# Values of two live pairs behind the scores, and a later turn for the first weights, in the sampled attention of a FoX and mLSTM decoder step

## The chip, the cores and the metric

The kernel runs on one core of one Trainium2 chip. The time is that of one execution on the device, in microseconds (us). The median of three runs is quoted, and one further execution was taken with the hardware profiler. TensorE (PE) does the matrix products, PEld is its loading of weights, VectorE (DVE) and ScalarE (ACT) work on vectors, GpSimd (POOL) does small vector work and issues the indirect transfers, and SyncE (SP) issues the plain ones.

## The reference: what is computed

One step of a decoder layer runs for 2048 prompt tokens and for eight sampled sequences of eight new tokens each. Both go through one input projection, forgetting attention (FoX, 8 heads of 64) beside an mLSTM matrix memory, one output projection, a norm, a squared-ReLU MLP (1024 to 4096 to 1024) and a second norm. All values are float32. The part that the change touches is the attention of the sampled tokens over 8192 cached positions, which lie in pages that a table names:

```python
def _fox_sample(q, k_new, v_new, logf_new, k_past, v_past, logf_past):
    ...
    s_past = jnp.einsum('bqhd,bkhd->bhqk', q, k_past).astype(jnp.float32) * scale
    s_past = s_past + Ln[..., :, None] + R[:, :, None, :]
    s_new = jnp.einsum('bqhd,bkhd->bhqk', q, k_new).astype(jnp.float32) * scale
    ...
    p = jax.nn.softmax(jnp.concatenate([s_past, s_new], axis=-1), axis=-1).astype(v_new.dtype)
    o = jnp.einsum('bhqk,bkhd->bqhd', p[..., :P], v_past) + jnp.einsum('bhqk,bkhd->bqhd', p[..., P:], v_new)
```

## The kernel before

The program is a main stream with a second one woven into it. The main stream has four parts in order: the input projection with the gates (to about 911 us of the profiled span), the prompt's attention (to about 1340), the output projection (to about 1600) and the MLP (to the end). Every main product is written as two or three matrix products of split operands (`mm3`, L156 to L159; the splitting is done by `split_hi` on ACT at L149 and `split_lo` on DVE at L152). In the MLP the products are named `ph` (hidden layer, evicted by ACT) and `py` (output, added by DVE at L1489).

The second stream is the attention of the eight sampled sequences. It is a Python generator, `sample_attention` (L1531), whose 294 steps (`step`, L1841) are emitted one at a time by `tick` (L129) when the main stream has issued a certain estimated time of matrix work, 5 us for a step in the last two parts. `beside` (L114) places what a step emits on PE, ACT and DVE behind the last main instruction of that engine. Within these bounds a scheduler, which reckons with its own model of the times, puts the instructions of each engine in their final order; instructions on POOL and SP are bound by their data and buffers alone. The stream stands still during the prompt's attention.

For each of the eight sequences (a batch `b` in the code, 32 steps long) the stream does the following.

- **Keys.** `k_gather` (L1666) issues one indirect gather of 512 KB of cached keys on POOL, `k_turn` (L1670) transposes it in place on DVE (L1674). In the later parts of the kernel six such pieces fit into a ring, so that a gather waits until the scores have read the piece whose place it takes.
- **Scores.** Every fourth step `qk_step` (L1683) multiplies the queries with four pieces (L1697, 16 products in 32 instructions of 32 columns, four of them side by side on the array), and DVE adds the forget terms and keeps maxima (L1704). This result is `sQ`.
- **Softmax.** At step 35 of the batch `softmax` (L1709) takes the scores of the new keys (L1716), the maximum, and eight exponentials on ACT (L1734), in four tiles `S` by two head groups, and two small ones of the new keys `Sn` (L1736).
- **Weights.** `weights(b, u, hg)` (L1758) turns a quarter `u` of one head group by four transposes on PE (L1766) into `sT`, and DVE and ACT copy them into `PTs` (L1768). There is one tile `PTs`, which serves four pairs of values.
- **New keys.** `softmax_new` (L1738) sums the exponentials on DVE and transposes those of the new keys (L1746, L1748), `v_new` (L1771) loads the new values (SP, 16 KB), `softmax_sum` (L1750) makes the sums of all pages by a product (L1754) and the reciprocal (L1756). All of it is used at the batch's last pair.
- **Values.** `v_gather` (L1775) issues two gathers of 512 KB, which the code calls a pair. There are two places for pairs: `vt`, and a second one (`vx` or `xr`) that exists only in the output projection and in the MLP, and is withdrawn at the ends of their blocks, where the same buffers take other data. `vx["live"]` lists the places in use, `vx["of"]` the pairs gathered. `pv_step` (L1792) multiplies one pair with the weights (L1809, eight products in 16 instructions) into the accumulator `sO`; the 16th pair of a batch (`kt` 15) adds the new values (L1815) and evicts. `pv_end` (L1820) transposes the result (L1824).

`sQ` and `sT` share a single PSUM buffer (tag `sX`): scores, transposes, new keys and sums take turns on it, each waiting until the one before was read. `at(n, first, of)` (L1833) gives `i` at step `first + i * of`, and nothing at the others. Before, the pair `p` is multiplied at step 38 + 2p: pairs with an even number meet a scores' step, those with an odd number stand two steps later. The first weights (`u` = 0) of a batch stand at its steps 36 and 37, the first in one step with the last pair of the batch before, the new keys at 37 and the sums at 40.

Of the kernel before, what the change touches and what calls it, by code (L numbers as in the profile page):

```python
# [1530 lines left out]
def sample_attention(tc, I, O, ps_, pps, cst, ident, sqk, dnl, dR, dmix, dqb, vx, kx, pe, ring_a):  # L1531
# [84 lines left out]
    for g in range(2):  # L1616
        p = pps.tile([32, 8, 64], F32, name="sT", tag="sX", bufs=1)
# [26 lines left out]
    def q_load(b):  # L1644
        qt = ps_.tile([128, 2, 16, 8], F32, name="qt", bufs=2)
        for n in range(2):
            SY.dma_start(qt[:, n].rearrange("p d t -> p (d t)"), dap(dqb, (n * NB + b) * 4096, [[0, 4], [128, 32], [1, 128]]))
        bn = ps_.tile([128, 2, 8], F32, name="bn", bufs=2)
        for hg in range(2):
            SY.dma_start(bn[:, hg], dap(dnl, hg * 4 * TOT + S + b * 8, [[TOT, 4], [0, 32], [1, 8]]))  # L1650
        state[b] = dict(qt=qt, bn=bn, U=[])
# [18 lines left out]
    def k_turn(n):  # L1670

        for i in range(2):
            x = piece(n)[:, i * 512:(i + 1) * 512]
            V.transpose(x, x)  # L1674
# [8 lines left out]
    def qk_step(g):  # L1683

        b, kt = divmod(g * 2, 16)
        z = state[b]
        rb = z["rb"]
        a0 = piece(4 * g)
        d = 1 if g < GA else (2 * (g - GA) + 1) % 3 - 2 * (g - GA) % 3
        pq = pps.tile([128, 2, 256], F32, name="sQ", tag="sX", bufs=1)  # L1690
        for hg in range(2):
            for db in range(2):
                for h4 in range(4):
                    hd = (hg * 4 + h4) * 2 + db
                    kv = bass.AP(tensor=a0.tensor, offset=a0.offset + hd * 32,
                                 ap=[list(a0.ap[0]), [d * 2048, 2], [512, 4], [1, 32]])
                    r = T.matmul(pq[h4 * 32:h4 * 32 + 32, hg].rearrange("p (k f c) -> p k f c", k=2, f=4), z["qb"][:, hd], kv,  # L1697
                                 start=(db == 0), stop=(db == 1), skip_group_check=True)
        if kt % 4 == 0:
            z["U"].append(ps_.tile([128, 2, 4, 4, 32], F32, name="S", tag="S", bufs=4))  # L1700
        for k in range(2):
            c = slice(k * 128, k * 128 + 128)
            for hg in range(2):
                V.tensor_tensor_reduce(out=z["U"][kt // 4][:, hg, :, kt % 4 + k], in0=pq[:, hg, c].rearrange("p (b t) -> p b t", t=32),  # L1704
                                       in1=rb[:, hg, c].rearrange("p (b t) -> p b t", t=32), scale=1.0, scalar=NEG,
                                       op0=OP.add, op1=OP.max, accum_out=z["mx"][:, hg, kt + k:kt + k + 1])
        return r
# [30 lines left out]
    def softmax_new(b):  # L1738

        z = state[b]  # L1740
        rs = z["rs"] = ps_.tile([128, 2], F32, name="rs", bufs=2)
        V.tensor_reduce(rs, z["rp"], axis=AX.X, op=OP.add)
        pn = z["pn"] = ps_.tile([8, 2, 32], F32, name="PTn", bufs=2)
        p = pps.tile([8, 2, 128], F32, name="sT", tag="sX", bufs=1)
        for hg in range(2):
            T.transpose(p[:, hg], z["Sn"][:, hg], ident)  # L1746
        for hg in range(2):
            A.copy(pn[:, hg].rearrange("p (h q) -> p h q", q=8), p[:, hg].rearrange("p (h g q) -> p g h q", g=4, q=8)[:, 0])  # L1748
# [9 lines left out]
    def weights(b, u, hg):  # L1758

        z = state[b]  # L1760
        if hg == 0:
            z["PT"] = ps_.tile([128, 2, 4, 4, 4, 8], F32, name="PTs", tag="PTs", bufs=1)
        PT = z["PT"]
        p = pps.tile([128, 4, 128], F32, name="sT", tag="sX", bufs=1)
        for f in range(4):
            T.transpose(p[:, f], z["U"][u][:, hg, f].rearrange("p k t -> p (k t)"), ident)  # L1766
        for f in range(4):
            (A.copy if f % 2 else V.tensor_copy)(PT[:, hg, f].rearrange("p g h q -> p h g q"),  # L1768
                                                 p[:, f].rearrange("p (h g q) -> p h g q", g=4, q=8))
# [22 lines left out]
    def pv_step(b, kt, after):  # L1792


        z = state[b]
        if kt == 0:
            z["po"] = pps.tile([128, 256], F32, name="sO", bufs=1)
        po = z["po"]
        pg = kt % 4
        vts = vx["of"].pop(b * 16 + kt)  # L1800
        vx["live"].pop(0)
        for n, f in enumerate((1, 0)):
            with ExitStack() as es:
                if after is not None:
                    es.enter_context(tc.issue_after(after.ins))
                for g in range(2):
                    for hg in range(2):
                        r = (g * 2 + hg) * 32
                        after_ = T.matmul(po[r:r + 32], z["PT"][:, hg, 2 * f + g, pg].rearrange("p h q -> p (h q)"),  # L1809
                                          vts[f][:, g, hg * 256:(hg + 1) * 256], start=(kt == 0 and n == 0),  # L1810
                                          stop=(g == 1 and kt == 15 and n == 1), skip_group_check=True)
            after = after_
        if kt == 15:
            for hg in range(2):
                T.matmul(po[hg * 32:hg * 32 + 32], z["pn"][:, hg], z["vn"][:, hg * 256:(hg + 1) * 256],  # L1815
                         start=False, stop=True, skip_group_check=True)
            z["os"] = ps_.tile([128, 256], F32, name="os", bufs=1)
            V.tensor_scalar(z["os"], po, z["rl"], None, op0=OP.mult)

    def pv_end(b):  # L1820
        z = state.pop(b)
        p = pps.tile([128, 2, 128], F32, name="sT", tag="sX", bufs=1)
        for c in range(2):
            T.transpose(p[:, c], z["os"][:, c * 128:(c + 1) * 128], ident)  # L1824
        for hh in range(2):
            s = slice(hh * 64, hh * 64 + 64)
            for c in range(2):
                for hg in range(2):
                    V.tensor_reduce(mixs[s, hg * 2 + c, b * 8:b * 8 + 8],
                                    p[s, c].rearrange("p (e g h q) -> p g h q e", e=2, g=2, q=8)[:, hg, 2 * c + hh],  # L1830
                                    axis=AX.X, op=OP.add)

    def at(n, first, of):  # L1833

        i, r = divmod(n - first, of)
        return i if r == 0 and i >= 0 else None
# [4 lines left out]
    def step(n):  # L1841
        after = None
        if n == 0:
            q_load(0)
        g, r = divmod(n - 2, 4)
        if 0 <= g < GA and r >= 2:
            k_turn(4 * g + 2 * r - 4)
            k_turn(4 * g + 2 * r - 3)
        if NA + 2 < n < 258:
            if n == NA + 3:  # L1850
                k_turn(NA)
            k_turn(n - 2)
        g = at(n, 6, 4)
        if g is not None and g < 64:
            after = qk_step(g)
        b = at(n, 35, 32)
        if b is not None and b < 8:
            softmax(b)
        p = at(n, 38, 2)
        if p is not None and p < 128:  # L1860
            pv_step(p // 16, p % 16, after)
        b = at(n, 69, 32)
        if b is not None:
            pv_end(b)
        b = at(n, 37, 32)
        if b is not None and b < 8:
            softmax_new(b)
            v_new(b)
        b = at(n, 40, 32)
        if b is not None and b < 8:  # L1870
            softmax_sum(b)
        for hg in range(2):
            u = at(n, 36 + hg, 8)
            if u is not None and u < 32:
                weights(u // 4, u % 4, hg)
        b = at(n, 30, 32)
        if b is not None and b < 7:
            q_load(b + 1)
        b = at(n, 3, 32)
        if b is not None and b < 8:  # L1880
            q_begin(b)
        g = at(n, 4, 4)
        if g is not None and g < 64:
            r_load(g)
        if n >= 35 and (n % 2 == 1 or not vx["live"]):
            while v_room():
                v_gather()
        g, r = divmod(n - 2, 4)
        if 0 <= g < GA and r < 2:
            k_gather(4 * g + 2 * r)  # L1890
            k_gather(4 * g + 2 * r + 1)
        if NA + 6 <= n < 256:
            k_gather(n)

    for n in range(294):
        yield 1
        step(n)
        if n == NA + 2:

            yield 3  # L1900
            for i in range(6):
                k_gather(NA + i)
                if i < 5:
                    yield 1
# [23 lines left out]
```

## Time and profile before

| what | value |
|---|---|
| median of three runs (lowest to highest) | 3322.77 us (3321.24 to 3331.57) |
| the profiled execution | 3348.73 us |
| its span, first to last instruction | 3347.0 us |
| mean granted clock of TensorE | 0.989 |
| DMA | 646.22 MB, 193 GB/s on average |
| gathers issued on POOL for keys and values | 256 and 256 |

The profile gives for each engine its busy time, for each wait the instruction that ended it, and the instructions in order of time. Instructions are named by line, engine, operation and tiles (`sO<-vt,PTs`: the accumulator from a gathered pair and the weights). The recorded ends of matrix products overlap their successors, so that their starts are the better measure. Every float32 product of the sampled stream shows as two instructions: 32 of them for a scores' step, 16 for a pair of values.

### The profile page before, as it was taken

How to read it: one execution, taken by the hardware profiler on the slowest of the kernel's cores; microseconds unless marked ns; L12 is line 12 of the kernel's file. 1: busy time of each engine (PE TensorE's matmuls, PEld its weight loads, DVE VectorE, ACT ScalarE, POOL GpSimd, SP SyncE). 2: the span in 40 equal slices, each digit the busy share in tenths (PEclk: the TensorE clock that was granted, in tenths of full speed). 3: DMA queues.
4: the chain of work that ended last, by engine and by line, in shares of the span. 5: the costliest groups of instructions: out<-in, count | busy, mean ns of one | idle time of the engine just before them, and what ended most of it. 6: DMA issues, size and time to landing. Idle time of an engine off the chain costs nothing. (4 is left out here: it accounts for less than half of the span.)

```text
span 3347.0 us, 57284 instructions
## 1 busy us (share of the span) xinstructions
PE 3224.8 (96%) x21420; PEld 2634.7 (79%) x21420; DVE 2130.2 (64%) x5161; ACT 1355.5 (40%) x2670; POOL 929.7 (28%) x1060
## 2 busy tenths in 40 slices
PE   9999999999999999999999999999999999999998
PEld 8998897787877777676777777777776777889997
DVE  6857567556478777656666667666676545755555
ACT  4443344334367777312332333232332333433332
POOL 0112122322344444465323324323243210100001
PEclk9999999999999999999999999999999999999999
DMA  5666765867642223787877768767668654542221
GB/s 174 167 190 190 220 205 189 288 215 226 220 122 84 77 82 114 246 274 242 296 241 250 247 232 298 253 224 270 211 238 304 198 172 142 160 138 79 89 85 66
DMA packets 427294, 646.22 MB, mean 193 GB/s; under 512 B 83149, under 2 KB 320017, under 8 KB 426121
## 3 DMA queue, kind: packets, MB, share of 16 engines
q1 hardware_dynamic: 350184, 363.09, 35.9%
q0 software_dynamic: 74304, 270.57, 22.0%
q10 hardware_dynamic: 2528, 8.91, 0.7%
q8 instruction: 169, 2.77, 0.3%
q14 instruction: 109, 0.89, 0.1%
HBM read 589.63 MB, written 52.83 MB: 192 GB/s over the span
## 5 line engine op out<-in xcount | busy, mean ns | idle before, releaser
L1489 DVE TENSOR_TENSOR y<-y,py 128x512 f32<-128x512 f32 x475 | 320.6, 682 | 313.5 <-PE py L159 276.9
L149 ACT ACTIVATE wh<-wr 128x1024 fp32r<-128x1024 f32 x268 | 279.4, 1056 | 523.7 <-PE py L159 207.1
L1668 POOL DMA_INDIRECT kT<-cache_k,idxK x256 | 269.1, 1051 | 725.5 <-PE sQ L1697 657.7
L159 PE MATMUL ph<-x1h,wl 128*128 128x512 f32 (+1 forms) x1280 | 452.6, 355 | 9.5 <-DVE wl L152 8.3
L157 PE MATMUL ph<-x1h,wh 128*128 128x512 f32 (+1 forms) x1280 | 454.7, 355 | 4.0 <-ACT wh L149 2.2
L158 PE MATMUL ph<-x1l,wh 128*128 128x512 f32 (+1 forms) x1280 | 454.5, 355 | 1.6 <-issue 1.6
L1674 DVE STREAM_TRANSPOSE kT<-kT 128x512 f32<-128x512 f32 x512 | 330.3, 685 | 182.2 <-DMA kT<-cache_k,idxK 171.6
L157 PE MATMUL py<-wh,h 128*128 128x512 f32 x1024 | 407.0, 400 | 4.4 <-DVE y L1487 2.3
L159 PE MATMUL py<-wh,h 128*128 128x512 f32 x1024 | 401.6, 393 | 1.0 <-issue 1.0
L158 PE MATMUL py<-wl,h 128*128 128x512 f32 x1024 | 401.5, 393 | 1.1 <-issue 1.0
L152 DVE TENSOR_TENSOR wl<-wr,wh 128x1024 fp32r<-128x1024 f32 x268 | 336.8, 1263 | 89.2 <-PE ph L159 35.2
L157 PE MATMUL pm<-whi,xhT 128*128 128x256 f32 (+2 forms) x1040 | 303.4, 292 | 3.2 <-issue 2.0
L158 PE MATMUL pm<-wlo,xhT 128*128 128x256 f32 (+2 forms) x1040 | 298.1, 287 | 0.0
L159 PE MATMUL pm<-whi,xlT 128*128 128x256 f32 (+2 forms) x1040 | 297.9, 286 | 0.0
L159 PEld LDWEIGHTS ph<-x1h,wl 128*128 128x128 f32 x1280 | 241.7, 189 | 45.6 <-DVE wl L152 10.5
L157 PEld LDWEIGHTS ph<-x1h,wh 128*128 128x128 f32 x1280 | 241.5, 189 | 42.0 <-issue 4.7
L158 PEld LDWEIGHTS ph<-x1l,wh 128*128 128x128 f32 x1280 | 241.8, 189 | 37.8 <-issue 6.4
L157 PEld LDWEIGHTS py<-wh,h 128*128 128x128 f32 x1024 | 192.5, 188 | 59.4 <-issue 11.9
L159 PEld LDWEIGHTS py<-wh,h 128*128 128x128 f32 x1024 | 192.5, 188 | 46.9 <-issue 5.8
L158 PEld LDWEIGHTS py<-wl,h 128*128 128x128 f32 x1024 | 192.7, 188 | 37.4 <-issue 2.3
L1785 POOL DMA_INDIRECT vt<-cache_v,idxV x158 | 161.5, 1022 | 201.0 <-PE sO L1809 140.2
L157 PEld LDWEIGHTS pm<-whi,xhT 128*128 128x128 f32 (+1 forms) x1040 | 199.1, 191 | 11.5 <-issue 8.8
(420 smaller groups left out, 6627.5 us busy)
## 6 DMA issues: line engine op xcount, KB each, us to landing
wr<-w SPq DMA_DIRECT2D x256, 512.0 KB
wra<-w_in SPq DMA_DIRECT2D x112, 512.0 KB
Rb<-dR SPq DMA_DIRECT2D x128, 128.0 KB
wr<-w_o SPq DMA_DIRECT2D x16, 512.0 KB
xr<-dmix SPq DMA_DIRECT2D x16, 512.0 KB
y<-x_prompt SPq DMA_DIRECT2D x16, 512.0 KB
dx<-y SPq DMA_DIRECT2D x16, 512.0 KB
xr<-dx SPq DMA_DIRECT2D x16, 512.0 KB
```

Of the source, the lines that this page charges most:

```text
L149: last["ACT"] = A.activation(dst, src, AF.Copy, scale=scale)
L152: r = (eng or V).tensor_tensor(dst, src, hi.bitcast(F32), op=OP.subtract)
L157: T.matmul(ps, wh, xh, start=first, stop=False)
L158: T.matmul(ps, wh, xl, start=False, stop=False)
L159: last["PE"] = T.matmul(ps, wl, xh, start=False, stop=stop)
L1489: V.tensor_tensor(y, y, ps, op=OP.add)
L1668: G.indirect_dma_start(out=piece(n), out_offset=None, in_=ck, in_offset=IO(ap=idxK[:, b, j // 2, j % 2:j % 2 + 1], axis=0))
L1674: V.transpose(x, x)
L1785: G.indirect_dma_start(out=vt.rearrange("p f c -> p (f c)"), out_offset=None, in_=cv, in_offset=IO(ap=idxV[:, b, (kt % 4) * 4 + kt // 4, f ...
```

## The change

`pv_step` returns its last instruction. At a step that is due for pair `p`, the pair is multiplied if that was not done before, and where `p` is even and pair `p` + 1 has been gathered already, that one is multiplied directly behind it, in the same step; a counter `done` keeps the odd step from doing it again. Where only one pair is live, everything stays at its step. Within a batch the first weights of both head groups stand at step 37 (before: 36 and 37); the later weights stay at their steps. The new keys and the new values' load go from step 37 to 39, the sums from 40 to 41. Within a step the order of the calls is as before: scores, softmax, values, `pv_end`, new keys, sums, weights, loads, gathers of values, gathers of keys.

```diff
@@ -1816,6 +1816,7 @@
             V.tensor_scalar(z["os"], po, z["rl"], None, op0=OP.mult)
+        return after
 
     def pv_end(b):
@@ -1857,22 +1858,29 @@
         p = at(n, 38, 2)
-        if p is not None and p < 128:
-            pv_step(p // 16, p % 16, after)
+        if p is not None and p < 128 and p >= done[0]:
+            after = pv_step(p // 16, p % 16, after)
+            done[0] = p + 1
+            if p % 2 == 0 and p + 1 in vx["of"]:
+                pv_step(p // 16, p % 16 + 1, after)
+                done[0] = p + 2
         b = at(n, 69, 32)
         if b is not None:
             pv_end(b)
-        b = at(n, 37, 32)
+        b = at(n, 39, 32)
         if b is not None and b < 8:
             softmax_new(b)
             v_new(b)
-        b = at(n, 40, 32)
+        b = at(n, 41, 32)
         if b is not None and b < 8:
             softmax_sum(b)
         for hg in range(2):
             u = at(n, 36 + hg, 8)
-            if u is not None and u < 32:
+            if u is not None and u < 32 and u % 4:
                 weights(u // 4, u % 4, hg)
+            u = at(n, 37, 32)
+            if u is not None and u < 8:
+                weights(u, 0, hg)
@@ -1892,6 +1900,7 @@
+    done = [0]
     for n in range(294):
         yield 1
         step(n)
```

## The prediction

> **What bounds the kernel now.** I read the page first, then the stretches in which the sampled stream runs, then the waits of TensorE and of its weight loads, and last the timeline of TensorE around single visits of the stream.
>
> ```profile
> PE 3224.8 (96%) x21420; PEld 2634.7 (79%) x21420; DVE 2130.2 (64%) x5161; ACT 1355.5 (40%) x2670; POOL 929.7 (28%) x1060
> ```
>
> TensorE is busy for 96% of the span and no other engine for more than 64%. The profiled execution took 3348.73 us, 1.7 more than its span and 26 (0.8%) more than the median of the three runs, 3322.77. The sum below is made in microseconds of the profiled execution; scaled by 0.992 it changes by 0.1, so I take it off the median as it is.
>
> ```profile
> 1340.00:2830.00 1490.00, 1443.37 (x8898) 1091.11 (x8899) 923.48 (x1794) 485.77 (x781) 514.11 (x478) 0.99 0.70 243
> ```
>
> The columns are the stretch, its length, the busy time (instructions) of PE, PEld, DVE, ACT and POOL, the granted clock, the DMA share and GB/s. From 1340 to 2830 the stream runs beside the output projection and the MLP, which is the only time in which two pairs can be live (before 911 there is one place, so no pair is joined there). There PE is busy for 97% of the time. So time is won here only by giving PE less to do, or less to wait for. The waits are small:
>
> ```profile
> PEld sO L1809 <- issue: 19.6, 58, 0.4
> PEld sT L1766 <- PE sO L1809: 5.0, 12, 0.5
> PE sT L1766 <- ACT PTs L1768: 2.9, 1, 2.9
> PE sT L1766 <- ACT S L1734: 2.2, 1, 2.2
> PE sO L1809 <- DMA vt<-cache_v,idxV: 1.5, 2, 0.8
> ```
>
> Each row is who waited, for whom, microseconds in all, times, the longest. PE waits 1.5 us for values that have not landed and 5.1 for the weights' softmax and copies. The first row says that values are entered 58 times with a short gap (0.34 us each) that nothing but the sequence explains: PE comes from other work, not from the scores. The second has 12 visits in which the next weights' transposes follow values directly.
>
> **What a visit costs.** The main matmuls start 0.227 us apart (13 steps in 2.95 us, first two rows below). Rows of the PE timeline are start, length, line, operation, count.
>
> ```profile
> 1907.72 0.39 PE L159 MATMUL ph<-x1h,wl 128*128 128x512 f32 x1
> ...
> 1910.67 0.39 PE L157 MATMUL ph<-x1h,wh 128*128 128x512 f32 x1
> 1910.98 1.93 PE L1697 MATMUL sQ<-kT,qb 128*32 128x256 f32 x32
> 1912.74 1.05 PE L1809 MATMUL sO<-xr,PTs 128*32 128x256 f32 x16
> 1913.71 0.50 PE L158 MATMUL ph<-x1l,wh 128*128 128x512 f32 x1
> ...
> 1915.69 0.39 PE L157 MATMUL ph<-x1h,wh 128*128 128x512 f32 x1
> ...
> 1920.23 0.39 PE L159 MATMUL py<-wh,h 128*128 128x512 f32 x1
> 1920.55 1.07 PE L1809 MATMUL sO<-vt,PTs 128*32 128x256 f32 x16
> 1921.55 0.50 PE L157 MATMUL py<-wh,h 128*128 128x512 f32 x1
> ...
> 1924.45 0.39 PE L157 MATMUL ph<-x1h,wh 128*128 128x512 f32 x1
> ```
>
> The even pair of this group stands behind the scores, the odd pair alone 10 us later. The lone visit, from 1920.23 to 1924.45, holds 13 main matmuls: 4.22 - 13 x 0.227 = **1.27 us**. The part beyond its 1.00 us of matmuls is a later entry (0.32 for 0.227), a later exit and a dozen main matmuls at 0.23 to 0.24. At nine places the schedule already puts both pairs behind the scores:
>
> ```profile
> 1983.40 0.39 PE L157 MATMUL ph<-x1h,wh 128*128 128x512 f32 x1
> 1983.72 1.93 PE L1697 MATMUL sQ<-kT,qb 128*32 128x256 f32 x32
> 1985.47 1.05 PE L1809 MATMUL sO<-xr,PTs 128*32 128x256 f32 x16
> 1986.33 1.05 PE L1809 MATMUL sO<-vt,PTs 128*32 128x256 f32 x16
> 1987.31 0.50 PE L157 MATMUL py<-wh,h 128*128 128x512 f32 x1
> ...
> 1989.25 0.40 PE L159 MATMUL py<-wh,h 128*128 128x512 f32 x1
> ```
>
> From main matmul to main matmul this visit is 3.91 us (1983.40 to 1987.31), the one with one pair 3.04 (1910.67 to 1913.71); the eight steps after take 1.94 and 1.98. The second pair thus costs 3.91 - 3.04 - 0.04 = **0.83 us**, and joining saves 1.27 - 0.83 = **0.44**.
>
> Three times in a batch the odd pair stands together with the transposes of the next weights, which the change leaves where they are:
>
> ```profile
> 1894.73 0.39 PE L159 MATMUL py<-wh,h 128*128 128x512 f32 x1
> 1895.05 1.07 PE L1809 MATMUL sO<-vt,PTs 128*32 128x256 f32 x16
> 1896.05 0.66 PE L1766 MATMUL sT<-ident,S 128*128 128x128 f32 x4
> ...
> 1898.84 0.39 PE L158 MATMUL py<-wl,h 128*128 128x512 f32 x1
> ...
> 1904.28 0.39 PE L159 MATMUL py<-wh,h 128*128 128x512 f32 x1
> 1904.51 0.60 PE L1766 MATMUL sT<-ident,S 128*128 128x128 f32 x4
> ...
> 1907.27 0.39 PE L158 MATMUL py<-wl,h 128*128 128x512 f32 x1
> ```
>
> With 11 main matmuls between its first and last row, the first visit is 4.11 - 11 x 0.227 = 1.61; the transposes alone, with as many, are 2.99 - 2.50 = 0.49. Afterwards there are 0.83 + 0.49 = 1.32, a saving of **0.29**.
>
> **The count.** I followed the PE timeline from 1380 to 2830, where odd pairs 23 to 127 run. Left out are nine that are joined already and those at the ends of blocks, where the second place is withdrawn (pairs 35, 37, 67, 99, 101). 21 of the rest stand alone and 14 with transposes (12 of these have the gap of the row above). The other entries among the 58 are even pairs, of the last batch above all, and visits cut in two.
>
> 21 x 0.44 = 9.2 and 14 x 0.29 = 4.1. Three irregular places (near 2080, 2120 and 2540, where the scores or both pairs stand apart) give 0.6 each, 1.8. Together 15.1 us.
>
> **Gathers.** Both pairs now free their places in one step, so POOL issues all four gathers of values behind one another, after the key gathers, and they must land before the next scores' step. The beginning of a batch shows that already, since there both pairs are joined today:
>
> ```profile
> 1767.76 1.93 PE L1697 MATMUL sQ<-kT,qb 128*32 128x256 f32 x32
> 1778.71 0.94 POOL L1785 DMA_INDIRECT vt<-cache_v,idxV  x1 [0.30 <-issue]
> 1783.35 1.93 PE L1697 MATMUL sQ<-kT,qb 128*32 128x256 f32 x32
> 2602.41 0.95 POOL L1785 DMA_INDIRECT xr<-cache_v,idxV  x1 [0.30 <-issue]
> 2612.19 1.07 PE L1809 MATMUL sO<-xr,PTs 128*32 128x256 f32 x16 [0.55 <-DMA xr<-cache_v,idxV]
> ```
>
> The last gather goes out 10.9 us after its visit's start (1767.76 to 1778.71). The last two rows are the slowest landing after which PE waited here: 9.8 us. So the second pair is there 21 us after the visit, and a scores' step comes every 27 us (two batches' first steps, 1767.76 and 1983.72, are eight steps apart). Only behind a batch's first visit is the next one early (1783.35, 15.6 us later). For five such pairs, which stand with transposes, I count no saving: 5 x 0.29 = 1.5. Worst, PE waits 3 us at each and the gain shrinks by 15. The key gathers keep their place ahead on POOL, since scores end before values; if the values went first, three more issues of 1.25 us each would delay the keys by some 4 us, for which DVE's transposes wait, and main additions behind them on DVE: bounded by a wait of PE of that length, which no row of a paired visit shows, so nothing is taken.
>
> **The moved steps.** The first weights' eight transposes, eight copies (ACT and DVE) stay the same in number; the first half moves by one step, so both halves stand in one step with the transposes of the old batch's output. The new-key sums (a DVE reduction, two transposes, two ACT copies, and SP's load of 16 KB of new values) move by two steps, the sum's matmuls and its reciprocal by one. All of these results are needed at the batch's last pair, 30 steps later, so they hide behind main matmuls: nothing, as a value. SP's load leaves the step in which it waited for the last pair's matmuls and passes no other load of the stream; loads of main weights stood behind it. All these users share one PSUM buffer:
>
> ```profile
> 1750.31 0.38 PE L1824 MATMUL sT<-ident,os 128*128 128x128 f32 x2
> 1755.80 0.38 PE L1746 MATMUL sT<-ident,Sn 128*8 128x128 f32 x2
> 1761.28 0.60 PE L1766 MATMUL sT<-ident,S 128*128 128x128 f32 x4
> ```
>
> These are the old batch's output, the new keys and the second half of the first weights; the first half stands before them. With the new keys' turn (1755.80) taken out, the scores' step at 1767.76 has one user fewer ahead, up to 6 us earlier. That helps gathers, not PE. Bounds: the waits of 5.1 us go (-5), or both halves, now in neighbouring turns, make PE wait as once today:
>
> ```profile
> 1461.21 1.11 PE L1766 MATMUL sT<-ident,S 128*128 128x128 f32 x4 [2.93 <-ACT PTs L1768]
> ```
>
> ```profile
> 1461.00:1464.40 3.40, 3.19 (x10) 2.71 (x11) 1.93 (x4) 1.40 (x2) 0.56 (x1) 0.50 0.60 171
> ```
>
> The stretch behind the wait has a granted clock (third figure from the end) of 0.50 for 3.4 us, which loses 1.7 more, 4.6 in all. The Trainium skill (TensorE: Matmul & The Clock Gate, "What's actually happening") has the clock fall after an idle window of about 3.4 us; by that alone a wait of 2.9 would cost 2.9. The trace shows the clock fallen after 2.93, and the measurement decides.
>
> **Sum.** -15.1 + 1.5 + 0 = -13.6 us: 3322.8 - 13.6 = **3309**, 0.41% faster. A difference under 0.3% (10 us) cannot be told from none here.
>
> **Rivals.** *Only the switches go* (or half of the pairs stay apart). Without the slow dozen, a lone visit costs 1.09 (1920.23 to 1921.55, less 0.227), a joined pair 0.87; 35 x 0.22 = 7.7, if the dozen stays as slow: 3315. The same follows if the schedule keeps every second odd pair alone because it reckons its gather late, and 3323 if it keeps all: then the change doesn't do what it says. For it: the schedule has joined only nine pairs so far. Against: those are emitted two steps apart today, and the slow dozen after the joined visit is no longer than after the single one. By the Trainium skill (TensorEngine Tiling (Array Packing), "Key Properties") a change of tiling mode drains the engine, and a saving of the drain alone would be this rival; the joined rows show more than that. Chance 0.26, 3313 to 3332.
>
> *The first weights stall.* Both halves share one buffer within a step, and ACT is on its eight exponentials just then. If PE waits as at 1461.21 in all eight batches, that is 8 x 4.6 = 37: 3346. From three batches on the gain is gone; from six on the kernel is slower by over 0.3%. For it: the first weights had a wait for the exponentials of 2.2 us in this stretch. Against: the rows above leave 5.5 to 6.5 us between users, and the wait for the new keys' exponentials leaves the chain. Chance 0.14, 3333 and above.
>
> *More than the sum*: waits of 5 to 10 us at the batches' beginnings go too, half clock included. 3297 to 3303, chance 0.08.
>
> **How the numbers follow.** The forecast has 0.52, from 3303 to 3312. Faster by over 0.3%: 0.52 + 0.08 = 0.60; within: 0.26; slower: 0.14. The range from 3298 to 3336 leaves out about 0.03 below and 0.12 above, the greater part of the slow rival.
>
> **What would show it.** Entries of values from other work fall from 58 to about 25; visits with 32 values' matmuls behind the scores rise from nine to over 35, at 3.9 us; waits for values' gathers stay under 5 us in all; PE's busy time in these stretches falls by some 13. A wait at L1766 or L1809 in most batches would prove me wrong, as would an odd pair still standing alone.

## The result and the profile after

| kernel | median of its runs (lowest to highest) | ratio to the kernel before, 95% interval |
|---|---|---|
| before | 3328.2 us (3321.24 to 3332.96, six runs) | |
| after | 3349.11 us (3335.46 to 3357.44, six runs) | 1.0055 [1.0039, 1.007] |

The change made the kernel slower by 0.55%, some 18 us; the forecast was a gain of 14 us. The profiled execution of after took 3335.46 us (span 3333.8), the shortest of its runs, while that of before had been longer than all of its timed runs. Read side by side they have the sign wrong. So a second profiled execution of the unchanged kernel (`e4`, span 3323.5 us, the same order of instructions on every engine) stands for before from here on, and one of the changed kernel (`e3`, span 3342.4 us) beside the first.

The page of after, and the stretch in which two pairs can be live (columns as in the prediction):

```profile
PE 3212.7 (96%) x21420; PEld 2641.3 (79%) x21420; DVE 2121.0 (64%) x5161; ACT 1358.7 (41%) x2670; POOL 931.0 (28%) x1060
```

```profile
1340.00:2830.00 1490.00, 1445.85 (x8932) 1108.88 (x8929) 922.52 (x1796) 487.47 (x780) 516.99 (x478) 0.99 0.70 244
```

The same stretch of the unchanged kernel's second profile:

```profile
1340.00:2830.00 1490.00, 1457.38 (x9005) 1106.24 (x9001) 941.44 (x1810) 493.31 (x787) 515.43 (x478) 0.99 0.70 245
```

PE is busy for 11.5 us less of these 1490 us, but it also gets through 73 matmuls less (8932 for 9005): part of the fall is not less work but more waiting. The waits of after show that both things happened:

```profile
PEld sO L1809 <- issue: 8.7, 25, 0.4
```

```profile
PE py L157 <- ACT h L149: 6.4, 1, 6.4
PE sT L1766 <- ACT PTs L1768: 6.1, 2, 4.0
PE sT L1766 <- DVE mixs L1830: 5.7, 1, 5.7
PE px L1284 <- DVE x1l L152: 5.0, 2, 3.8
PE sO L1809 <- DMA vt<-cache_v,idxV: 3.9, 5, 1.4
PE px L1284 <- DMA xr<-dx: 3.4, 2, 3.0
...
PE sO L1809 <- DMA xr<-cache_v,idxV: 1.7, 3, 1.1
```

The reader is to see two things. Entries of values from other work fell from 58 to 25 (56 in `e4`), just as forecast, and waits for gathered values are 5.6 us in eight places. But there are new or longer waits, the longest of 4.0 to 6.4 us, at one or two places each, and they are of different kinds: a main operand that ACT has split late (`h`, L149), a buffer that ACT has not yet copied (L1768), the output of the sequence before, which DVE has not yet reduced (L1830). None of them repeats from batch to batch.

Where a joined visit stands, it costs what was forecast (timeline of PE in after, start and length in front):

```profile
1813.06 0.39 PE L159 MATMUL ph<-x1h,wl 128*128 128x512 f32 x1
1813.38 1.93 PE L1697 MATMUL sQ<-kT,qb 128*32 128x256 f32 x32
1815.13 1.05 PE L1809 MATMUL sO<-vt,PTs 128*32 128x256 f32 x16
1815.99 1.05 PE L1809 MATMUL sO<-xr,PTs 128*32 128x256 f32 x16
1816.97 0.50 PE L157 MATMUL py<-wh,h 128*128 128x512 f32 x1
```

3.91 us from main matmul to main matmul. There are 33 such visits (nine before), and not all that were joined in the code stay joined. Here the schedule has put main work between the two pairs, and the first pair's values come late besides:

```profile
1827.62 1.93 PE L1697 MATMUL sQ<-kT,qb 128*32 128x256 f32 x32
1830.19 1.07 PE L1809 MATMUL sO<-vt,PTs 128*32 128x256 f32 x16 [0.64 <-DMA vt<-cache_v,idxV]
1833.68 1.07 PE L1809 MATMUL sO<-xr,PTs 128*32 128x256 f32 x16
```

The span can be split into three: the gaps of PE of over 0.15 us, half of the time in which its clock is granted at 0.50, and the rest, which is nearly all work at full pace. They are added up over all of PE's rows and all of the clock's records within the span.

| kernel, its profile | span | gaps | lost to half clock | rest |
|---|---|---|---|---|
| before, second profile (e4) | 3323.5 | 90.3 | 37.8 | 3195.3 |
| after | 3333.8 | 103.5 | 43.2 | 3187.1 |
| after, second profile (e3) | 3342.4 | 111.5 | 48.2 | 3182.7 |
| joined pairs alone (e1) | 3335.5 | 108.7 | 39.1 | 3187.6 |
| moved steps alone (e2) | 3348.8 | 108.0 | 44.7 | 3196.1 |

The joining took 8 to 13 us of work away (rest: 3195.3 to 3187.1, 3182.7 and 3187.6), and the gaps grew by 13 to 21 us. The moved steps alone change no work (3196.1), and add the gaps all the same. Part of the time at half clock falls into gaps and into the span's end, where PE has nothing to do; counted only while PE is busy, it costs 24.7 us in `e4`, 33.0 in after, 36.8 in `e3`, 28.0 in `e1` and 36.7 in `e2`. One profile is one execution: the rest of the first profile of before was 3205.5, 10 us more than that of the second with the same instructions in the same order, and the profiled execution of after lay 14 us below the median of its runs, that of `e1` 9 us above. So the sizes are good to some microseconds, not better, and the verdicts below go by the ratios.

### The profile page after: what moved, and what is told of

Read it like the earlier page. It is cut to its first block, busy times and chain, and to the rows that moved or that the text cites. A ratio compares the mean times of both kernels' runs of the same rounds, so it can differ in the third digit from the quotient of the medians.

```text
span 3333.8 us, 57289 instructions
## 1 busy us (share of the span) xinstructions
PE 3212.7 (96%) x21420; PEld 2641.3 (79%) x21420; DVE 2121.0 (64%) x5161; ACT 1358.7 (41%) x2670; POOL 931.0 (28%) x1060
## 5 line engine op out<-in xcount | busy, mean ns | idle before, releaser
L149 ACT ACTIVATE wh<-wr 128x1024 fp32r<-128x1024 f32 x268 | 278.3, 1056 | 449.7 <-PE py L159 213.6
L1451 ACT ACTIVATE hq<-ph 128x512 f32<-128x512 f32 (+1 forms) x160 | 82.5, 516 | 313.6 <-PE ph L159 242.6
```

Of the source, the lines that this page charges most:

```text
L149: last["ACT"] = A.activation(dst, src, AF.Copy, scale=scale)
L1451: A.activation(hq, ps, AF.Relu)
```

## The experiments

All kernels compute the whole result. The median and the ratio are those of five rounds against the kernel before.

| run | what differs from the kernel before | median, us | ratio, 95% interval |
|---|---|---|---|
| e3 | the whole change, again | 3353.36 | 1.0081 [1.0063, 1.0099] |
| e4 | nothing | 3328.65 | 0.9998 [0.9984, 1.0012] |
| e1 | pairs joined, no step moved | 3327.96 | 1.0003 [0.9991, 1.0015] |
| e2 | steps moved, no pair joined | 3349.41 | 1.005 [1.003, 1.0069] |
| e5 | of the moved steps, the first weights | 3340.32 | 1.0029 [1.0013, 1.0046] |
| e6 | of the moved steps, new keys and sums | 3342.16 | 1.0036 [1.0022, 1.0049] |
| e7 | moved steps in batches 0 and 1 | 3336.58 | 1.0012 [0.9996, 1.0028] |
| e8 | moved steps in batches 2 to 7 | 3338.43 | 1.003 [1.0016, 1.0045] |
| e17 | moved steps in batches 0, 1, 3, 5, 7 | 3346.09 | 1.0047 [1.0031, 1.0062] |
| e18 | moved steps in batches 2, 4, 6 | 3345.05 | 1.0045 [1.0029, 1.0061] |
| e9 | whole change, norm vectors held back | 3346.3 | 1.0042 [1.003, 1.0054] |
| e10 | moved steps, norm vectors held back | 3344.0 | 1.0039 [1.0026, 1.0052] |
| e11 | joined pairs, norm vectors held back | 3328.93 | 0.999 [0.9981, 0.9999] |
| e12 | norm vectors put first, nothing else | 3340.15 | 1.003 [1.0018, 1.0042] |
| e13 | norms' stores issued by POOL, nothing else | 3331.01 | 1.0006 [0.9993, 1.0019] |
| e14 | e10 with those stores | 3342.19 | 1.0038 [1.0024, 1.0051] |
| e15 | e9 with those stores | 3337.68 | 1.0033 [1.0017, 1.0049] |
| e16 | e11 with those stores | 3330.76 | 1.0004 [0.9991, 1.0016] |

**The change taken apart.** Theory M: the moved steps cost. Theory G: the gathers of joined pairs come late. In e1 the three moved steps stand where they stood before; e2 leaves the joining out of the change, these lines above all:

```diff
-            if p % 2 == 0 and p + 1 in vx["of"]:
-                pv_step(p // 16, p % 16 + 1, after)
-                done[0] = p + 2
```

> Only the joining of two pairs, with the first weights, the new keys and the sums at their old steps. If the moved steps are what costs time (theory M), this is the sum of the prediction without them: 10 to 15 us faster than before, ratio 0.996. If the joined pairs cost it, because four gathers of values in a row land late and TensorE waits for them at half a clock afterwards (theory G), this is as slow as the whole change, ratio 1.004 to 1.007, and its waits for gathered values in the output projection and the MLP are over 5 us in its profile.

> Only the moved steps, pairs as before. Theory M: 0.5 to 1% slower than before, with waits of TensorE at the transposes of first weights of 4 us or more, each with 3.4 us of half clock behind it. Theory G: within 0.2% of before.

> The changed kernel once more, unchanged, on the same chip as the others. Both theories: ratio 1.004 to 1.007. Its profile, a second one, should show where a usual execution differs from the profiled one of the result, which was shorter than all of its timed runs: theory G expects more waits for gathered values, theory M more at the transposes; TensorE's busy time about 3212 us in both.

> The kernel before once more, unchanged. Ratio 1.000 within 0.2%. A second profile of it, since the one that the prediction read was 0.8% longer than the median of the runs: if that excess was in TensorE's waits, this span is near 3325 with TensorE idle for about 100 us instead of 122.

The whole loss is there without any joining (1.005), and none without moved steps (1.0003). So M holds as to which part of the change loses. The waits that M expected are not there: PE waits at first weights in two batches of e2's profile, 3.8 us in batch 0 and 2.2 us in batch 2, each in pieces of 2.3 us or less, and not 4 or more. And the joining does not win what it was to win either, though it takes 7.7 us of work off PE: the gaps of e1 are 18 us longer than those of e4.

For this lost gain the profiles speak for G. From the output projection to the end of the stream, PE waits for gathered values 12.2, 13.8 and 13.7 us in the three kernels with joined pairs and no moved steps (e1, e11, e16), and 2.1 to 6.0 us in those with neither (before, e4, e12, e13). That is some 7 us more, of the 8 to 10 us of work that these three save there.

**Which of the moved steps?** F: the first weights, whose halves now meet in one step. K: new keys and sums. D: neither; each new order of the steps re-times all queues, and the parts don't add up.

```diff
-        b = at(n, 37, 32)
+        b = at(n, 39, 32)
...
-        b = at(n, 40, 32)
+        b = at(n, 41, 32)
```

These lines are e6; e5 has the lines on `weights` of the change instead. In e7 and e8 the whole set of moved steps applies to n under 98 (batches 0 and 1) or from 98 on.

> Only the first weights of both head groups at step 37, new keys and sums at their old steps. Theory F (the first weights' place itself makes TensorE wait): about 20 us slower than before, ratio 1.005 to 1.007. Theory K (the later new keys and sums do, because their vector work then stands in front of the main stream's on VectorE): within 0.2% of before. Theory D (no one place: each new order re-times all queues, and its waits with the half clock behind them are spread): between the two, and the parts do not add up.

> Only the new keys and the load of new values two steps later and the sums one step later; first weights at 36 and 37. Theory F: within 0.2% of before. Theory K: ratio 1.005 to 1.007, with the wait of 2.8 us of the mLSTM's product behind the sums near 850 us that all three profiles with the moved steps have. Theory D: between the two.

> All moved steps, but for the first two batches alone, which begin beside the input projection (before 911 us). If the loss of the moved steps is made there (the 2.8 us wait near 850, a wait of the scores for their transposed keys near 580, one half-clock period more in each profile), ratio 1.003 to 1.006; otherwise within 0.2% of before.

> All moved steps, but for the six later batches alone, which begin beside the output projection and the MLP. If the loss is made there, ratio 1.003 to 1.006; otherwise within 0.2% of before. With theory D both halves lose some, and the two losses need not add up to the 0.5% of the moved steps together.

Each half loses (0.29% and 0.36%), together 0.50%; neither F nor K holds by itself. Early and late batches, 0.12% and 0.30%, do add up within their intervals; the 0.12% alone is not clear of nothing.

**Does SP's queue carry it?** Between the same two main matmuls (the 12376th and the 13200th, the beginning of the MLP's third block) e4 takes 231 us and e7 231, but e8, e2 and e6 take 245 to 248. (The first profile of before takes 236 here, and e1, which loses nothing, 242: a long stretch is not yet a loss.) There, in after, ACT stands still for weights that land late. Timeline of ACT in after:

```profile
2431.11 2.99 ACT L149 ACTIVATE wh<-wr 128x1024 fp32r<-128x1024 f32 x3
2450.05 1.06 ACT L149 ACTIVATE wh<-wr 128x1024 fp32r<-128x1024 f32 x1 [15.95 <-DMA wr<-w]
...
2452.29 0.63 ACT L149 ACTIVATE h<-hq 128x512 fp32r<-128x512 f32 x1
```

and the timeline of PE, which waits for that last row:

```profile
2452.97 0.79 PE L157 MATMUL py<-wh,h 128*128 128x512 f32 x1 [6.39 <-ACT h L149]
```

The last split, `h`, stands behind the split of weights (2450.05) in ACT's order, and with it waits for a load that it doesn't need. In e4 ACT waits for the same load too, 7.51 us, but there the split of `h` stands ahead of it:

```profile
2434.85 0.64 ACT L149 ACTIVATE h<-hq 128x512 fp32r<-128x512 f32 x1
...
2447.15 1.06 ACT L149 ACTIVATE wh<-wr 128x1024 fp32r<-128x1024 f32 x1 [7.51 <-DMA wr<-w]
```

So what differs most is ACT's order. The load itself goes out at 2435.46 in e4 and at 2439.15 in after, 3.7 us later, and lands 11.7 us and 10.8 us after that. SP's timeline just ahead of it, in after:

```profile
2435.72 0.33 SPq L145 DMA_DIRECT2D g<-ln_g  x1
2438.02 0.33 SPq L145 DMA_DIRECT2D b<-ln_b  x1
2439.15 0.38 SPq L1255 DMA_DIRECT2D wr<-w  x1
...
2441.39 1.19 SPq L1272 DMA_DIRECT2D xr<-dx  x2
2442.64 0.56 SPq L1255 DMA_DIRECT2D wr<-w  x1
```

and in e4:

```profile
2418.28 0.94 SPq L1272 DMA_DIRECT2D xr<-dx  x2
2428.61 0.34 SPq L145 DMA_DIRECT2D g<-ln_g  x1
2430.31 0.33 SPq L145 DMA_DIRECT2D b<-ln_b  x1
```

The reader is to see that the same loads have changed places: the next block's rows (`xr<-dx`, L1272) stand ahead of the norm's vectors (L145) in e4 and behind them in after, though the change touches neither. Theory Q: this order is the loss. The lines below are the hold of e9 to e11; e12 does the reverse to the kernel before (the row loads follow the vectors):

```diff
-                    gb = vecs(2)
+                    with ExitStack() as es_l:
+                        if ci < 3:
+                            es_l.enter_context(tc.issue_after(last_x[1 - len(CB[ci + 1])].ins))
+                        gb = vecs(2)
```

> The changed kernel, complete, with the norm vectors' loads (L145) held behind the second load of the next block's rows (L1272) on SP's queue at each block's start, which is where the kernel before has them; the changed kernel has them ahead of all four row loads at the third block. Theory Q (the loss comes from SP's order of loads at the blocks' starts, which the moved steps shift): ratio falls from 1.0055-1.0081 to 1.001-1.003, and the stretch of main matmuls 12376-13200 from 243-251 us to 232-238 us. Theory D (any new order re-times all queues; no one place): 1.0045-1.008 as before, the stretch above 240 us.

> The moved steps alone, with the same hold of the norm vectors' loads behind the second row load (moves alone had them ahead of all four at the second and the third block). Q: ratio 1.001-1.003 (from 1.005), stretch 12376-13200 232-238 us (from 245). D: 1.004-1.006, the stretch above 240 us.

> The joined pairs alone, with the same hold (pairs alone had the vectors ahead of all four row loads at the second and the third block). Q: the joining's 9-10 us of TensorE, which waits ate, come out: ratio 0.997-0.999 (pairs alone: 1.0003), faster than both kernels. D: 0.999-1.0015.

> The kernel before, complete, with nothing of the change: only the norm vectors' loads are put ahead of the four row loads on SP's queue at the starts of blocks two to four. Q: ratio 1.002-1.004, the stretch 12376-13200 above 238 us (from 231-236). D: 0.9985-1.0015.

e12, which has nothing of the change, loses 0.30%. That this is the order of the loads alone is not shown: e12 executes PE's instructions in another order than before at over 100 places, and its third block's stretch takes 234 us, where Q had over 238. The hold may give something back to the joined pairs: e11 is at 0.999 where e1 was at 1.0003, with intervals that overlap. But Q doesn't explain the loss. e1 has the vectors ahead of the rows as after has, and loses nothing. The expectation for e10 was wrong in its premise: moved steps alone had the row loads in front already, and the executed order of e10 is that of e2 on every engine. Its 1.0039 is a second measurement of the same program (1.005 the first time). And e9, where the order was mended, still takes 241 us in the third block's stretch and stays at 1.0042.

**Stores that wait for POOL.** Theory S: SP's store of `y_prompt` waits for POOL's add (L177) ahead of weight loads. The stores of the two norms go out from POOL instead, directly behind the add:

```diff
-            SY.dma_start(dx1[t * 128:(t + 1) * 128], xs[t])
+            G.dma_start(dx1[t * 128:(t + 1) * 128], xs[t])
...
```

> The kernel before, complete, with the norms' stores (L1340, L1497) issued by POOL, right behind the add that they wait for (L177), instead of by SP. Theory S (in the changed kernels SP's store of y_prompt waits up to 19 us for POOL's add, and weight loads queued behind it reach ACT's split up to 10 us late): the kernel before has such waits too, of up to 14-18 us, but other loads behind them: 0.998-1.001. Theory D: 0.998-1.003, any order re-times everything.

> The moved steps alone, norm vectors' loads behind the second row load, and the norms' stores issued by POOL. Theory S together with Q: the rest of the loss (1.0039) goes: 0.999-1.0015 against before, the stretch of main matmuls 12376-13200 230-236 us (from 245.6), ACT's waits for weights there (L150 for wr) under 12 us (from 30). Theory D: 1.003-1.005.

> The changed kernel, complete, with the norm vectors' loads behind the second row load and the norms' stores issued by POOL. S with Q: 0.997-1.001 against before (from 1.0042), the joining's 10 us of TensorE come out. D: 1.003-1.006.

> The joined pairs alone with both edits of SP's queue. S with Q: 0.996-0.999 against before, the fastest of all. D: 0.998-1.002.

S falls. With these waits gone, the moved steps are still at 1.0038, and the stretch takes 249 us; ACT still waits 21 us for weights in it, where S had under 12. e13 adds something else: it executes PE's instructions in another order than the kernel before at over 80 places, and loses nothing that can be measured (1.0006).

**Which batches?** Theory P: the softmax of batches 2, 4 and 6 comes 9 to 11 steps ahead of a block's start, and moved steps cost there alone. In e17 and e18 the moved steps apply to the other batches or to these:

```diff
-        b = at(n, 37, 32)
+        b = at(n, 39 if ((n - 35) // 32 not in (2, 4, 6)) else 37, 32)
...
```

> The moved steps alone, and only in batches 0, 1, 3, 5 and 7, whose softmax does not fall just ahead of a block's start; batches 2, 4 and 6 as before. Theory P (the place: the softmax of batches 2, 4 and 6 comes 9 to 11 steps ahead of the first block's, the third's and the rest of the blocks' loads, where ACT has no time to spare; moved steps cost there and nowhere else): 0.999-1.0015, and the stretches of main matmuls 8700-9500 and 12376-13200 at 228-231 and 230-236 us as in the kernel before. Theory D (any moved step costs alike): 1.0025-1.0035.

> The moved steps alone, and only in batches 2, 4 and 6. P: 1.0035-1.005, nearly all of the loss of the moved steps, the stretches at 232-236 and 241-249 us. D: 1.0015-1.0025, three eighths of it.

P falls too. Either set of batches loses as much as both together (0.47%, 0.45%; both 0.39 to 0.50%). And e17 loses in the third block's stretch although the moved steps of batch 6, the nearest ones, stand there as before. The waits of PE in this stretch, first e4 (2399 to 2630 us):

```profile
PE ph L159 <- DVE wl L152: 3.2, 1, 3.2
```

then e17 (2411.5 to 2656.5):

```profile
PE py L157 <- DVE y L1487: 5.2, 2, 2.8
PE px L1284 <- DMA xr<-dx: 2.7, 1, 2.7
PE sQ L1697 <- DVE kT L1674: 2.4, 1, 2.4
PE ph L159 <- DVE wl L152: 2.2, 1, 2.2
```

then moved steps alone, e2 (2412 to 2657.5):

```profile
PE ph L157 <- ACT wh L149: 5.2, 2, 3.4
PE ph L159 <- DVE wl L152: 1.6, 3, 0.6
```

and e6 (2410.5 to 2658.5):

```profile
PE sQ L1697 <- issue: 8.6, 2, 8.3
PE px L1284 <- DMA xr<-dx: 5.6, 1, 5.6
```

The place is the same, but the wait is another one in every kernel: an eviction by DVE, a split by ACT, a load of rows, and 8.3 us ahead of scores for which the view names no releaser. Followed back along the engines, though, the longest of them end alike, at a load of main weights that lands late. In e6:

```profile
2509.97 1.06 ACT L149 ACTIVATE wh<-wr 128x1024 fp32r<-128x1024 f32 x1 [7.04 <-DMA wr<-w]
2512.23 0.69 DVE L152 TENSOR_TENSOR h<-hq,h 128x512 fp32r<-128x512 f32 x1 [8.28 <-ACT h L149]
2512.84 2.48 DVE L1674 STREAM_TRANSPOSE kT<-kT 128x512 f32<-128x512 f32 x4
2514.24 3.41 PE L1697 MATMUL sQ<-kT,qb 128*32 128x256 f32 x32 [8.29 <-issue]
```

DVE's split of `h` waits for ACT, which has waited for the weights, the key transposes stand behind it, and the scores start when these have begun. In e2 the 3.4 us wait stands behind the same thing:

```profile
2523.41 1.06 ACT L149 ACTIVATE wh<-wr 128x1024 fp32r<-128x1024 f32 x1 [7.93 <-DMA wr<-w]
```

In e17 such waits of ACT (8.71 us at 2513.14 and 3.97 us at 2518.17, both for weights) precede the two waits for DVE's eviction. The one wait of over 2 us in e4 ends at a gather of keys instead. So the place is tight, and a new order finds something there that stands behind a late load. That is D's picture. ACT's waits for weights alone do not sort the kernels, however: they are 23 us in e4's stretch, 30 to 31 in e2's and e6's, but 21 in e14's, which is as long. That D holds as a law, that any new order costs, has e13 against it, as far as moving the stores did not itself win what the new order lost.

**One wait followed to its cause.** In the input projection the moved steps of batch 1 end in the same wait of PE, 0.4 to 2.8 us: it is in all eleven profiles in which a step of batch 1 is moved, and in none of the other nine. PE in e2:

```profile
858.83 0.51 PE L1754 MATMUL sT<-rs,sel 128*128 128x1 f32 x4
...
862.17 0.66 PE L784 MATMUL mm<-ident,qk 128*128 128x128 f32 x4 [2.84 <-DVE qi L773]
```

DVE in e2, just before:

```profile
853.50 1.30 DVE L1674 STREAM_TRANSPOSE kT<-kT 128x512 f32<-128x512 f32 x2 [3.74 <-DMA kT<-cache_k,idxK]
856.99 1.31 DVE L1674 STREAM_TRANSPOSE kT<-kT 128x512 f32<-128x512 f32 x2 [2.19 <-DMA kT<-cache_k,idxK]
858.21 2.11 DVE L152 TENSOR_TENSOR wlo<-wra,whi 128x1024 fp32r<-128x1024 f32 x1
860.25 1.29 DVE L1674 STREAM_TRANSPOSE kT<-kT 128x512 f32<-128x512 f32 x2
861.47 0.65 DVE L773 SCALAR_TENSOR_TENSOR qi<-mm,qi 128x512 f32<-128x512 f32 x1
```

In e4 the product that follows the sums waits for nothing:

```profile
852.51 0.60 PE L784 MATMUL mm<-ident,qk 128*128 128x128 f32 x4
```

In e2 DVE has key transposes ahead of `qi`, which wait 3.7 and 2.2 us for their gathers; `qi` comes late by that, and PE with it. The moved step itself (`sT<-rs,sel`, 0.51 us) costs nothing: it has only shifted what stands before what on DVE. What it costs beyond its own length is not shown. Between the 3332nd and the 5600th main matmul, where this lies, e7, e2 and e17 take 428.6, 430.1 and 432.5 us and e4 425.4; but the first profile of before takes 427.8, and e1 and e11, which move no step, 428.1 and 428.6.

## Why the prediction was wrong, point by point

- **What bounds the kernel** was right: PE is busy for 96% of the span after as before. But "the waits are small" was read as if they stayed so.
- **The joined pair**, 0.44 us each: right in mechanism as to PE's work, smaller in sum. The visits of after take the times that the prediction read in before, 3.91 us for the joined one. But 24 were joined anew (33 less nine) for the 35 counted, since the schedule keeps some apart, as at 1830 us above. 24 x 0.44 are 10.6 us. Measured from the output projection's first main matmul to the end of the stream (the 8685th to the 13845th), without gaps and half clock, the time falls from 1411.5 us in e4 to 1399.7 in after (-11.8) and 1401.3 in e1 (-10.2). Forecast were 15.1. As a gain of the kernel this term failed altogether: joining alone is at 1.0003 [0.9991, 1.0015], and in the same stretch of its profile the gaps grow from 26.7 us to 42.7.
- **Gathers**, 1.5 us taken off the gain: with the moved steps, waits for gathered values are 5.6 us in after (5.5 in e4), within the bound. Without them they are 12.2 to 13.8 us (e1, e11, e16), so for the joining by itself this term was some 7 us and not 1.5.
- **The moved steps**, "nothing, as a value": this step failed, and it decides the sign. They cost 0.39 to 0.50% (e10, e2, the same order of instructions twice), 13 to 17 us, where the sum had 0. Their own work does hide, as the prediction argued: in the stretch above, the time without gaps and half clock is 1411.9 and 1411.6 us in e2 and e10, 1411.5 in e4. The gaps are what grows, from 26.7 us to 39.4 and 36.2. The bounds (-5 to +37) held the loss, but for another reason than the one given.
- **The rival "the first weights stall"** had the right sign and, for the most part, the wrong mechanism. By it, one wait recurs in each batch, and new keys and sums cost nothing. In after PE waits at the first weights of two batches, 3.5 us in batch 0 and 5.7 in batch 2 (e4: 1.5 and 1.0), and at those of the other six not over 0.15 us. The two waits at L1766 for `PTs`, 6.1 us, stand at later weights, which the change leaves at their steps; so does the row at 1461.21 that the prediction priced the rival by (the last quarter of batch 1). And new keys and sums without the first weights (e6) lose 0.36%.
- **"Only the switches go"**, 3315 us, and **"more than the sum"**: neither time came. The first rival's 7.7 us lie near what joining took off PE by accident, since that was 24 pairs at some 0.44 and not 35 at 0.22. Its other condition, that the schedule keeps pairs apart, came true for about a third of them.
- **What would show it** came true in part: 58 entries went to 25, and a joined visit takes 3.91 us. But there are 33 of them and not over 35, waits for gathered values are 5.6 us and not under 5, and an odd pair does still stand alone (1833.68), which was named as a sign of being wrong. All of these test the work that PE was relieved of. None of them tested whether the gaps elsewhere stay as they are.
- **The step that was missing**: a scheduler orders the queues for the whole program, so a step moved in one place changes DVE's, ACT's and SP's order in others. The profile of before gave no row for this, but the range should have had a case for it, slower by up to 0.5%.

What stays open: why moved steps lose in the versions tried (seven different sets, 0.12 to 0.50%, all but e7 clear of nothing), while an order changed by other means lost 0.30% once (e12) and nothing once (e13). The runs show a tight place, the third block's start, where PE's longest waits stand behind late loads of main weights or rows, and one chain through DVE in the input projection. They don't show one queue that carries the rest, and no run takes the late loads away to see what is left.

The best version is e11, joined pairs without moved steps and with the vectors held back: 0.999 [0.9981, 0.9999]. That is 3 us, and with the stores moved as well (e16, 1.0004) it was not seen. So no version beats the kernel before by an amount worth the edit.

## What to carry to other kernels

Where one engine is busy for 96% of the time, what it is relieved of comes out only if the gaps stay as they are; measure the gaps, the time at half clock and the rest apart, and compare executions of one program first, since two profiles of the kernel before differ by 23 us in span. Where a scheduler orders the queues, a step that hides its own work is not thereby free to move: compare the executed order on all engines, and give the range a case for what has changed places without being touched. When parts of a change lose as much singly as together, look for a tight place that any of them disturbs, and follow each long wait back over the engines: a wait put down to ACT or DVE may stand behind a load.

## What the hardware showed that I had not expected

A long wait of PE costs more than its own length. Stretches of after, the wait of 6.39 us and what follows it (the granted clock is the third figure from the end):

```profile
2446.10:2452.97 6.87, 0.48 (x4) 0.06 (x2) 0.67 (x3) 2.85 (x5) 0.00 (x0) 0.68 1.01 366
2452.97:2459.00 6.03, 6.03 (x20) 5.05 (x21) 5.91 (x11) 0.97 (x3) 0.00 (x0) 0.51 0.61 231
```

For 6.0 us after the wait the clock is at 0.51, although PE is busy all the time: 3 us more, 9.4 in all. The records have the clock at 0.50 from 2.0 us after the wait's beginning, and for 10.24 us, three times the 3.41 us that the prediction read behind a wait of 2.93 us. The Trainium skill (TensorE: Matmul & The Clock Gate, "What's actually happening") describes windows of some 3.4 us after which the clock falls or rises. The lengths seen here, 3.41, 6.83 and 10.24 us, are one, two and three of them, so this trace agrees with it. The length of the wait does not set the price alone: in the same execution a wait of 5.69 us (at 1524.03) is followed by 3.41 us at half clock, and one of 2.51 us (at 794.42) by none.
